# Six of eight GLU chunks as sevenfold products, mixing between pairs, and a paced LayerNorm

## The chip, the cores and the metric

One core of a Trainium2 chip runs one inference step. The metric is device time in microseconds (us) from launch to end; the kernel before takes 1117.84 us (median of 3 runs, 1117.55 to 1118.63). Engines by their names in the profile: PE (TensorE, matrix products; PEld is its weight loading), DVE (VectorE), ACT (ScalarE), POOL (GpSimd) and SP (SyncE, here only a queue that issues DMAs). Each engine executes its own instructions in the order in which the program lists them.

## The reference

Tokens are 16 meta tokens, 1024 prompt tokens and 64 sample tokens (8 sequences of 8), with 1024 channels.

```
h = RMSNorm(x);  z = h @ w_in            # 7 column groups of 1024
a_val, a_gate, a_silu, p_in, p_silu, g_a, g_b = split(z)
u = a_val * sigmoid(a_gate)                              # GLU
c = causal depthwise conv of u, width 31, history from state_conv
c = silu(LayerNorm(c)) * silu(a_silu);   br_a = c @ w_conv_out
pooled = trailing mean over 2/4/8/16 positions of p_in - p_in   (4 channel groups)
q = (pooled @ w_pool_mix per group) * pool_scale * silu(p_silu); br_b = q @ w_pool_out
y = RMSNorm(x + (sigmoid(g_a)*br_a + sigmoid(g_b)*br_b) @ w_out)
```

The ends of u and of p_in are outputs too (the new states).

## The kernel before, in words

**Products.** Channels lie on the 128 partitions, so 1024 of them are 8 chunks. Tokens lie along the free axis in two halves of 552 (8 meta, 512 prompt, 32 sample); outputs without meta tokens have 544. A half is two units of 276 or 272 columns, each in one PSUM bank. For float32 accuracy each operand is split into a high part and a low part, and a product is three matmuls: high x high, high x low, low x high. The low part is made in one of two ways. `split` (L118) casts on ACT and subtracts on DVE. `split_dma` (L123) casts and negates on ACT, and an accumulating DMA issued by POOL adds the source.

**Plain and sevenfold.** A plain block is one chunk of 128 output channels: 2 halves x 8 input chunks x 3 x 2 units = 96 matmuls. `seven` (L437) computes two output chunks x two token halves together, by a scheme of seven products in place of eight; each product has 24 matmuls, so a pair of chunks takes 168 instead of 192. It needs sums of weight blocks (`Weights.sum`, L401, on DVE), sums of input blocks (`make_t`, L690), a copy of the first product (y, L453) and two corrections on DVE (L470, L479). Loads, sums and splits of weights run 8, 5 and 4 products ahead (`prepare`, L419).

**Stages.** First six pool-input chunks are multiplied with the raw input, while the input's RMSNorm is computed. Then come 18 plain blocks (`BLOCKS`, L49): two pool inputs, and gate and value of the 8 GLU chunks. Then 16 pairs (`ORDER`, L50): pool silu (q), the two merge gates (b, a), conv silu (s). Then the mixing (L821 to L842) of the pooled chunks with `w_pool_mix`, the pool projection (L862, `ppo`), the conv projection (`pco`) and the output projection (`pwo`).

**Beside the products.** Pool windows (`pool_work`, L508) and the conv (`Conv`, L582: 31 taps of 1024 elements per chunk, then the sample part) run on DVE. They wait in a list `todo`; the planner adds estimated costs (`t_op`, L59) to one clock for DVE and a fixed time per product to one for PE, and `fill` takes items from the list until the DVE clock has caught up:

```
    def fill(until=None):
        while todo and (until is None or clock["dve"] < until):
            ...
            cost, run = todo[0].popleft()
            clock["dve"] += cost
            run()
```

`step` advances the clock of PE and runs what `defer` has put off by some steps; `spend` books other work on DVE. What is left in the list after the pairs is emitted at L816. Conv results and their sum go to DRAM (`put`, L643); the pool projection loads them again and computes the LayerNorm at fixed places between its blocks (L869 to L894): mean, centring and squares at blocks 1 to 3, variance and root at block 5, `branch_a` (L854) at blocks 5 to 7. In that stage SP issues, block by block, the load of a weight block, the load of a gate half pair `lb` and the store of the products `d_tb` (L863 to L879).

Of the kernel before, what the change touches and what calls it, by code (L numbers as in the profile page):

```python
# [43 lines left out]
NSLOT, NWS, NOP, NZ = 35, 10, 6, 8  # L44
# [4 lines left out]
BLOCKS = "p6 p7 " + " ".join(f"g{i} v{i}" for i in range(8))  # L49
ORDER = "q0 q1 q2 q3 b0 b1 b2 b3 a0 a1 a2 a3 s0 s1 s2 s3"  # L50
# [18 lines left out]
def hybrid_trunk_kernel(  # L69
# [40 lines left out]
    ones32 = const.tile([P, P], F32, name="ones32")  # L110
# [67 lines left out]
    def totals(s, n, name):  # L178
        hl = [slot(f"sum{x}_{name}", (2, n), F32R) for x in "hl"]
        split(hl[0], hl[1], s)  # L180
        out = slot(f"total_{name}", (2, n))
# [149 lines left out]
    for k in range(NK):  # L331
        dve.scalar_tensor_tensor(xs[k], xs[k], col(OFF_NG, k), rms, ALU.mult, ALU.mult)
        split_x(0, (k,), split)
    plain1(1)
    plain1(2)
    keep_raw(1, 1, outs[1])
    split_x(1, (0, 1), split)
    plain1(3)
    keep_raw(2, 1, outs[2])
    split_x(1, (2, 3), split)  # L340
    plain1(4)
    keep_raw(3, 1, outs[3])
    split_x(1, (4, 5), split)
    plain1(5)
    keep_raw(4, 1, outs[4])
    split_x(1, (6, 7), split)
# [90 lines left out]
    def seven(w, units, put):  # L437
# [46 lines left out]
    d_gate, d_sga, d_sgb, d_sa, d_c, d_tb = (  # L484
        dram.tile([NK, P, 2, H2], F32, name=f"d_{x}") for x in ("gate", "sga", "sgb", "sa", "c", "tb")
    )
    d_pool = dram.tile([NK, P, 2, 2, H2], F32, name="d_pool")
# [14 lines left out]
    def pool_load(j):  # L502
        if j < NK:
            lraw[j] = [half(f"lraw{j}{h}") for h in range(2)]
            for h in range(2):
                sp.dma_start(out=lraw[j][h], in_=d_raw[j][:, h])

    def pool_work(j):  # L508
# [3 lines left out]
        def start():  # L512
# [3 lines left out]
            sp.dma_start(out=es[:, :, :PB], in_=spool[j])  # L516
            for h in range(2):
# [11 lines left out]
            defer(2, lambda: sp.dma_start(out=o_ps[j], in_=es[:, :, DS:]))  # L529
# [10 lines left out]
        def last():  # L540
            e, es, s, ss = cur
            dve.scalar_tensor_tensor(s[:, META:], s[:, META:], 1.0 / w, e[:, META:], ALU.mult, ALU.subtract)  # L542
            dve.scalar_tensor_tensor(ss[:, :, PB:], ss[:, :, PB:], 1.0 / w, es[:, :, PB:], ALU.mult, ALU.subtract)

        def out(h):
            s, ss = cur[2:]
            o = slot(f"poolop{j}{h}", (2, H2), F32R)
            b = slice(h * DB // 2, (h + 1) * DB // 2)
            split_dma(o[:, 0, :HP], o[:, 1, :HP], s[:, META + h * HP : META + (h + 1) * HP])
            split(v3(o[:, 0, HP:], DS), v3(o[:, 1, HP:], DS), ss[:, b, PB:])  # L550
            defer(3, lambda: sp.dma_start(out=d_pool[j][:, h], in_=o.bitcast(F32)))
# [7 lines left out]
        for h in range(2):  # L559
            work.append((0.25, lambda h=h: out(h)))  # L560
# [5 lines left out]
    def gate_pair(i, base, name, func, dst):  # L566
        def put(b, h, z):
            o = z
            if not b:
                o = half2(f"z{name}{i}{b}{h}", H2)  # L570
            act.activation(o, z, func)
            act.dma_start(out=dst[2 * i + b][:, h], in_=flat(o))

        return [(w_in[base + 2 * i], w_in[base + 2 * i + 1], f"{name}{i}", UNITS2, put)]
# [3 lines left out]
    d_e = dram.tile([NK, P, TP], F32, name="d_e")  # L578
    d_es = dram.tile([NK, P, DB, DS], F32, name="d_es")


    class Conv:  # L582
        fetched = []
# [16 lines left out]
        def fetch(self):  # L600
            i = self.i
            e = self.e = slot(f"ce{i}", (CB + TP,))
            es = self.es = st.tile([P, DB, ES], F32, tag="ces", name=f"ces{i}", bufs=2)
            pool.memset(e[:, :CB], 0.0)
            sp.dma_start(out=e[:, CB:], in_=d_e[i])
            sp.dma_start(out=es[:, :, :CB], in_=sconv[i])
            sp.dma_start(out=es[:, :, CB:], in_=d_es[i])
            defer(3, lambda: sp.dma_start(out=o_cp[i], in_=e[:, TP : TP + CB]))
            defer(3, lambda: sp.dma_start(out=o_cs[i], in_=es[:, :, DS:]))
# [28 lines left out]
        def store(self):  # L638
            Conv.fetched.remove(self)
            Conv.more()  # L640
            defer(2, self.put)

        def put(self):  # L643
            sp.dma_start(out=d_c[self.i], in_=self.c)
            if not csum:
                csum.append(dram.tile([P, 2, H2], F32, name="d_csum"))
                sp.dma_start(out=csum[0], in_=self.c)
            else:
                pool.dma_start(out=csum[0], in_=self.c, accum_op=ALU.add)

    chunks = []

# [3 lines left out]
    def put_block(kind, i, h, ps):  # L656
# [7 lines left out]
        else:  # L664
            z = sg.pop(h)
            dve.tensor_tensor(v3(z, HT // 2), ps, v3(z, HT // 2), ALU.mult)
            spend(HT)
            m, p, s = parts4(z)

            def out():  # L670
                sp.dma_start(out=d_e[i][:, META + h * HP : META + (h + 1) * HP], in_=p)
# [448 lines left out]
```

## Time and profile before

| | |
|---|---|
| median of 3 runs | 1117.84 us |
| the profiled execution's own time | 1117.58 us |
| its span, first to last instruction | 1115.8 us |
| PE busy | 990.3 us, 89% |
| DVE busy | 731.9 us, 66% |
| ACT, POOL busy | 469.1 us, 174.4 us |
| granted TensorE clock, mean | 0.951 |

Busy time is the union of an engine's instructions. A row of a group of instructions gives the line, engine, operation, written tile<-read tiles, shapes and count, then busy time and mean duration, then the idle time of the engine ahead of them and what ended it. In the table by stage the busy times are those of PE, PEld, DVE, ACT and POOL in this order, each with its count of instructions in brackets. A granted clock of 1.00 is the full 2.4 GHz. In rows by time the first number is the start in us from the span's beginning, the second the length of the merged instructions.

### The profile page before, as it was taken

What the parts mean: (1) busy time and instruction counts of PE and PEld (TensorE: products, weight loads), DVE (VectorE), ACT (ScalarE), POOL (GpSimd) and SP (SyncE); (2) the same over time, 40 slices, a digit from 0 to 9 for tenths busy, and PEclk for the clock granted to TensorE, in tenths of its full rate; (3) what the DMA queues carried; (4) which work ended last, traced back from release to release, by engine and by line L of the source; (5) the groups of instructions that cost most, each with busy time, mean ns of one, the idle gap of its engine ahead of it and who ended that gap; (6) DMA issues with size and microseconds to landing.
All of it is one profiled execution on the core that took longest, in us unless ns stands there. A gap on an engine that the chain in (4) does not pass through costs nothing. (4 is left out here: it accounts for less than half of the span.)

```text
span 1115.8 us, 18229 instructions
## 1 busy us (share of the span) xinstructions
PE 990.3 (89%) x7176; PEld 962.1 (86%) x7176; DVE 731.9 (66%) x945; ACT 469.1 (42%) x791; POOL 174.4 (16%) x211
## 2 busy tenths in 40 slices
PE   9978885789999899999999999759967649999997
PEld 9978885789999899999999999758967649998885
DVE  7473542698998999999898998354434443355333
ACT  7635432313325665655455555234236452225111
POOL 0001211111213222322222232001011121000000
PEclk9999998789999999999999999979998969999999
DMA  9217999996559797989879796999346569544222
GB/s 318 73 48 165 198 214 201 205 233 162 119 143 204 171 234 185 225 200 207 197 176 239 180 224 145 309 343 320 101 107 184 161 187 279 153 155 150 77 94 95
DMA packets 144805, 205.94 MB, mean 185 GB/s; under 512 B 59216, under 2 KB 60624, under 8 KB 144720
## 3 DMA queue, kind: packets, MB, share of 16 engines
q1 hardware_dynamic: 104832, 128.42, 38.6%
q0 software_dynamic: 28368, 54.01, 28.0%
q10 hardware_dynamic: 11520, 22.35, 6.0%
q8 instruction: 56, 0.92, 0.3%
q14 instruction: 29, 0.24, 0.1%
HBM read 99.37 MB, written 55.27 MB: 139 GB/s over the span
## 5 line engine op out<-in xcount | busy, mean ns | idle before, releaser
L621 DVE SCALAR_TENSOR_TENSOR c<-ce,pv,c 128x1024 f32<-128x1024 f32 x240 | 307.9, 1283 | 5.9
L149 PE MATMUL pv<-hx,w_v 128*128 128x276 f32 x768 | 105.1, 299 | 20.7 <-DMA w_v<-raw_v 20.7
L149 PEld LDWEIGHTS pv<-hx,w_v 128*128 128x128 f32 x768 | 103.2, 197 | 21.8 <-DMA w_v<-raw_v 21.8
L149 PE MATMUL pco<-cx,w_co 128*128 128x272 f32 x768 | 101.6, 295 | 22.4 <-DMA w_co<-raw_co 11.4
L149 PEld LDWEIGHTS pco<-cx,w_co 128*128 128x128 f32 x768 | 100.1, 194 | 23.8 <-DMA w_co<-raw_co 12.1
L149 PE MATMUL pg<-hx,w_g 128*128 128x276 f32 x768 | 104.5, 298 | 14.2 <-DMA w_g<-raw_g 14.2
L149 PEld LDWEIGHTS pg<-hx,w_g 128*128 128x128 f32 x768 | 103.0, 197 | 14.9 <-DMA w_g<-raw_g 14.9
L149 PE MATMUL ppo<-q,w_po 128*128 128x272 f32 x768 | 100.0, 293 | 6.4 <-DMA w_po<-raw_po 6.0
L149 PEld LDWEIGHTS ppo<-q,w_po 128*128 128x128 f32 x768 | 99.2, 192 | 7.2 <-DMA w_po<-raw_po 6.4
L993 PE MATMUL pwo<-wo,mx 128*128 128x512 f32 x336 | 79.3, 394 | 0.0
L993 PEld LDWEIGHTS pwo<-wo,mx 128*128 128x128 f32 x336 | 63.1, 188 | 14.8
L149 PE MATMUL pp<-xg,wh_p 128*128 128x276 f32 x384 | 66.8, 296 | 7.8 <-ACT rawp L259 7.7
L149 PEld LDWEIGHTS pp<-xg,wh_p 128*128 128x128 f32 x384 | 56.5, 194 | 8.7 <-ACT rawp L259 7.9
L149 PE MATMUL pmix<-lp,m 128*128 128x272 f32 x192 | 31.5, 329 | 16.7 <-DVE lg L840 10.6
L878 DVE TENSOR_TENSOR lb<-ppo,lb 128x544 f32<-128x544 f32 x16 | 11.5, 722 | 52.0 <-DMA lb<-d_sgb 40.2
L149 PEld LDWEIGHTS pmix<-lp,m 128*128 128x128 f32 x192 | 29.6, 225 | 18.5 <-issue 10.0
L149 PE MATMUL pp<-xg,wl_p 128*128 128x276 f32 x192 | 40.7, 294 | 0.0
L663 ACT ACTIVATE zg<-pg 128x552 f32<-128x552 f32 x16 | 9.9, 628 | 68.8 <-PE pg L149 63.3
L119 ACT CAST mx<-lga 128x544 fp32r<-128x544 f32 x16 | 10.3, 646 | 61.0 <-DVE lga L954 61.0
L1012 DVE TENSOR_TENSOR xr<-pwo,xr 128x1024 f32<-128x1024 f32 (+1 forms) x9 | 10.0, 1106 | 39.4 <-DMA xr<-in_xres 24.8
L124 ACT CAST poolop<-pw 128x512 fp32r<-128x512 f32 x16 | 9.9, 618 | 60.8 <-DVE pw L542 33.1
L975 ACT ACTIVATE sq<-xr 128x1024 f32<-128x1024 f32 (+1 forms) x9 | 8.7, 965 | 63.5 <-DVE xr L1012 63.5
(328 smaller groups left out, 1918.2 us busy)
## 6 DMA issues: line engine op xcount, KB each, us to landing
d_pool<-poolop SPq DMA_DIRECT2D x16, 544.0 KB, 7.9
lp<-d_pool SPq DMA_DIRECT2D x16, 544.0 KB, 7.6
lraw<-d_raw SPq DMA_DIRECT2D x16, 276.0 KB, 7.5
d_c<-c SPq DMA_DIRECT2D x8, 544.0 KB, 5.8
lg<-d_gate SPq DMA_DIRECT2D x16, 272.0 KB, 6.1
lb<-d_sgb SPq DMA_DIRECT2D x16, 272.0 KB, 6.4
lc<-d_c SPq DMA_DIRECT2D x8, 544.0 KB, 9.1
d_tb<-lb SPq DMA_DIRECT2D x16, 272.0 KB, 2.2
```

Source lines behind the costliest of these rows:

```text
L119: act.copy(dst_h, src)
L124: act.copy(dst_h, src)
L149: pe.matmul(out[:, u, : hi - lo], w(k, a), xs(k, b)[:, lo:hi], start=first and k == ks[0] and i == 0, stop=last and k == ks[-1] and i == 2 ...
L621: dve.scalar_tensor_tensor(c, s, wk, c, ALU.mult, ALU.add)
L663: act.activation(v3(sg[h], HT // 2), ps, AF.Sigmoid)
L878: dve.tensor_tensor(of_half(lb[h]), ps, of_half(lb[h]), ALU.mult)
L975: act.activation(sq[:rows, c], xr[:, c], AF.Square, accum_out=a1 if ns[0] else a0)
L993: pe.matmul(ps[:, n - ns[0]], x(k), wo[k][n][w], start=(k == 0 and s == 0), stop=(k == NK - 1 and s == len(passes) - 1),)
L1012: dve.tensor_tensor(v3(xr[:, c], 512), ps[:, : len(ns)], v3(xr[:, c], 512), ALU.add)
```

## The change

Of the 18 plain blocks six stay: gate and value of GLU chunks 0 and 1, and the two pool inputs. The other six GLU chunks run as three pairs of gates and three of values. The pool-silu results stay in SBUF; the mixing of a group runs in four parts between the products of the next pair, and its results go through DRAM to the pool projection. Weights of plain blocks are all split by `split`. The conv chunks that finish after the pairs are kept in SBUF; the LayerNorm becomes items of the list `todo`, behind the conv. States of samples are loaded into contiguous tiles, and POOL copies them to and from the tiles with history. The copy y stands after the second product. The normalisation of the input is interleaved with the raw blocks.

```diff
-NSLOT, NWS, NOP, NZ = 35, 10, 6, 8
+NSLOT, NWS, NOP, NZ = 34, 10, 6, 11
-BLOCKS = "p6 p7 " + " ".join(f"g{i} v{i}" for i in range(8))
-ORDER = "q0 q1 q2 q3 b0 b1 b2 b3 a0 a1 a2 a3 s0 s1 s2 s3"
+BLOCKS = "g0 v0 p6 p7 g1 v1"
+ORDER = "g1 v1 g2 v2 g3 v3 q0 q1 q2 q3 b0 b1 b2 b3 a0 a1 a2 a3 s0 s1 s2 s3"
...
     plain1(1)
+    keep_raw(1, 1, outs[1])
     plain1(2)
-    keep_raw(1, 1, outs[1])
+    norm_x((0,))
+    keep_raw(2, 1, outs[2])
+    norm_x((1, 2, 3))
...
-        y = bank2(f"py_{name}")
-        act.copy(y[:, :, :n], x[:, :, :n])
-        yield
         v = bank2(f"pv_{name}")
         product_of(v, "q3", "T3", True, False)
         yield
+        y = bank2(f"py_{name}")
+        act.copy(y[:, :, :n], x[:, :, :n])
         fill(clock["pe"])
         product_of(x, "q2", "T2", False, False)
...
+            lraw[j].append(st.tile([P, DB, PB], F32, tag="pst", name=f"pst{j}", bufs=3))
+            sp.dma_start(out=lraw[j][2], in_=spool[j])
...
-            sp.dma_start(out=es[:, :, :PB], in_=spool[j])
+            stage = lraw[j][2]
...
+            pool.tensor_copy(es[:, :, :PB], stage)
+            pool.tensor_copy(stage, es[:, :, DS:])
...
+    def value_pair(i):
+        def put(b, h, z):
+            glu(2 * i + b, h, glu_gate.pop((2 * i + b, h)), z)
+            if (b, h) in ((0, 1), (1, 0)):
+                Conv(2 * i + b)
...
+            work.insert(20, (0.0, self.join))
+            work.insert(0, (0.0, self.sample_load))
...
+        def join(self):
+            i, state = self.i, self.state
+            es = self.es = st.tile([P, DB, ES], F32, tag="ces", name=f"ces{i}", bufs=1)
+            pool.tensor_copy(es[:, :, :CB], state)
+            pool.tensor_copy(es[:, :, CB:], self.new)
+            pool.tensor_copy(state, es[:, :, DS:])
+            defer(1, lambda: sp.dma_start(out=o_cs[i], in_=state))
...
-            ops[n + 1].split()
+            ops[n + 1].split(split)
+            spend(512, 2)
...
+        if mix:
+            mix.split(0)
+            mix.split_w()
+            mix.load(1)
+        if n + 1 == len(pairs):
+            for j, t in enumerate((1, 1, 2, 2, 3, 4, 5, 5)):
+                if j > 1:
+                    defer(t - 2, lambda j=j: load_q(j)) if t > 2 else load_q(j)
+                defer(t, lambda j=j: split_q(j))
+            defer(1, po[0].load)
+            defer(3, po[1].load)
+            defer(5, lambda: po[0].split(split))
         next(after, None)
         next(cur)
-        if nxt:
-            next(nxt)
+        if mix:
+            mix.gate(*mix.part(0, 0))
+        next(nxt, None)
+        if mix:
+            mix.gate(*mix.part(0, 1))
+            mix.split(1)
+        next(cur)
+        if mix:
+            mix.gate(*mix.part(1, 0))
...
-    fill()
...
+    Conv.keep = True
...
+    def centre(i):
+        if i < NK:
+            dve.tensor_tensor(conv[i], conv[i], norm["mean"], ALU.subtract)
+            norm[i] = slot("vsum" if i == 0 else f"csq{i}", (2, H2))
+            act.activation(norm[i], conv[i], AF.Square)
+        if i > 1:
+            dve.tensor_tensor(norm[0], norm[0], norm.pop(i - 1), ALU.add)
...
+    finish_a = [(5.0, root)] + [(5.2, lambda i=i: branch_a(i)) for i in range(NK)]
+    squares_ = [(2.7, lambda i=i: centre(i)) for i in range(NK + 1)]
+    squares_.append((1.3, lambda: begin_totals(0, "var", finish_a)))
+    push([(1.3, lambda i=i: sum_rest(i)) for i in range(NK)] + [(1.3, lambda: begin_totals("sum", "mean", squares_))])
...
-        (po + co)[d + 1].split()
+        (po + co)[d + 1].split(split)
+        spend(512, 2)
         for h in range(2):
             ps = gemm_half(f"ppo{d}", po[d], q, h, NK)
             dve.tensor_tensor(of_half(lb[h]), ps, of_half(lb[h]), ALU.mult)
+            spend(H2)
...
-            step(6.0)
...
+            step(2 * T_PRODUCT)
+            if d == 0:
+                load_conv(h * 4, h * 4 + 4)
+                if h:
+                    load_sum()
+            else:
+                fill(clock["pe"])
+    while todo or due:
+        fill()
+        step(0.0)
...
-            co[d + 1].split(split_dma if d < 4 else split)
+            co[d + 1].split(split)
```

## Rows read from the trace of the kernel before

**Rows 1.** Stages: window, length, busy us by engine, granted clock, DMA share, GB/s
```profile
95.50:363.00 267.50, 232.63 (x1725) 230.83 (x1726) 185.26 (x252) 86.78 (x158) 52.88 (x64) 0.94 0.89 186
363.00:713.50 350.50, 342.53 (x2690) 341.00 (x2689) 315.54 (x366) 195.22 (x325) 88.54 (x104) 0.99 0.85 201
713.50:762.00 48.50, 31.40 (x193) 29.40 (x191) 20.52 (x29) 12.56 (x21) 1.72 (x2) 0.79 0.98 352
762.00:893.80 131.80, 103.73 (x784) 102.03 (x784) 55.34 (x61) 55.90 (x74) 16.64 (x20) 0.92 0.58 166
893.80:1011.40 117.60, 101.57 (x769) 100.37 (x770) 53.59 (x76) 38.04 (x61) 11.16 (x13) 0.92 0.67 189
1011.40:1115.80 104.40, 96.40 (x416) 77.76 (x415) 42.47 (x87) 22.58 (x70) 0.00 (x0) 0.99 0.30 102
```

**Rows 2.** Waits of all engines: who, on whom, us in total, times, longest
```profile
DVE pws L537 <- DMA pes<-in_spool: 34.8, 7, 11.7
...
PE pv L149 <- DMA w_v<-raw_v: 20.7, 5, 7.9
...
PE pg L149 <- DMA w_g<-raw_g: 14.2, 3, 7.8
...
PE pmix L149 <- DVE lg L840: 10.6, 4, 9.5
```

**Rows 3.** TensorE in time, blocks and a pair: start, us, instruction
```profile
90.81 0.77 PE L149 MATMUL pp<-hx,w_p 128*128 128x276 f32 x4 [0.73 <-ACT w_p L124]
...
263.89 12.38 PE L149 MATMUL pg<-hx,w_g 128*128 128x276 f32 x96
276.11 12.38 PE L149 MATMUL pv<-hx,w_v 128*128 128x276 f32 x96
...
402.89 3.16 PE L149 MATMUL px_q<-tT,woq_q 128*128 128x272 f32 x24
...
423.99 0.78 PE L149 MATMUL px_q<-tT,woq_q 128*128 128x272 f32 x5
```

**Rows 4.** Tile c, the conv's sum: durations ns, first and last start
```profile
L634 DVE TENSOR_REDUCE c<-tap x32: 669/670/672, 266.8 to 704.6; 128x16 f32<-128x496 f32 x32
```

**Rows 5.** Groups of VectorE and ScalarE: busy us, mean ns, idle time before
```profile
L621 DVE SCALAR_TENSOR_TENSOR c<-ce,pv,c 128x1024 f32<-128x1024 f32 x240 | 307.9, 1283 | 5.9
...
L446 ACT COPY c_b<-px_b 128x544 f32<-128x544 f32 x8 | 4.9, 614 | 15.7 <-PE px_b L149 15.7
...
L479 DVE SCALAR_TENSOR_TENSOR c_b<-pv_b,c_b 128x544 f32<-128x544 f32 x4 | 2.9, 725 | 7.8 <-PE pv_b L149 7.8
...
L405 DVE TENSOR_TENSOR q_b<-q_b,a_b 128x512 f32<-128x512 f32 x4 | 2.8, 692 | 0.1
```

**Rows 6.** VectorE in time, an eviction of the pool projection and the LayerNorm's branch
```profile
799.48 0.72 DVE L878 TENSOR_TENSOR lb<-ppo,lb 128x544 f32<-128x544 f32 x1 [9.06 <-DMA lb<-d_sgb]
...
855.69 1.28 DVE L856 TENSOR_TENSOR lc<-lc,ir_c 128x1088 f32<-128x1088 f32 x1
858.34 1.36 DVE L859 TENSOR_TENSOR lc<-lc,lsa 128x544 f32<-128x544 f32 x2 [1.37 <-ACT lc L857]
...
862.88 0.73 DVE L859 TENSOR_TENSOR lc<-lc,lsa 128x544 f32<-128x544 f32 x1 [1.98 <-ACT lc L857]
...
864.96 0.72 DVE L859 TENSOR_TENSOR lc<-lc,lsa 128x544 f32<-128x544 f32 x1
```

**Rows 7.** SyncE's queue in time, the stores of block 2 of the pool projection
```profile
800.24 11.98 SPq L879 DMA_DIRECT2D d_tb<-lb  x2
```

**Rows 8.** ScalarE in time, the totals of mean and variance
```profile
773.59 1.08 ACT L119 CAST sumh_m<-lcsum 128x1088 fp32r<-128x1088 f32 x1
777.14 1.13 ACT L188 COPY total_m<-pt_m 128x544 f32<-128x544 f32 x2 [2.47 <-PE pt_m L187]
...
840.54 1.08 ACT L119 CAST sumh_v<-vsum 128x1088 fp32r<-128x1088 f32 x1
```

**Rows 9.** GpSimd's groups, the memset ahead of a conv chunk
```profile
L604 POOL MEMSET ce<- 128x30 f32 x8 | 3.3, 411 | 16.9 <-DMA poolop<-pw 9.5 <-DMA out<-pe 7.3
```

More of the change, by code (lines that the diff above doesn't have):

```diff
@@ L541, in last @@
             e, es, s, ss = cur
[L542 to L551, printed above, removed]
+            o = slot(f"pool{j}", (2, H2))
+            dve.scalar_tensor_tensor(
+                o[:, :, :HP], v3(s[:, META:], HP), 1.0 / w, v3(e[:, META:], HP), ALU.mult, ALU.subtract
+            )
+            for h in range(2):
+                c = slice(h * DB // 2, (h + 1) * DB // 2)
+                dve.scalar_tensor_tensor(
+                    v3(o[:, h, HP:], DS), ss[:, c, PB:], 1.0 / w, es[:, c, PB:], ALU.mult, ALU.subtract
+                )
+            defer(1, lambda: sp.dma_start(out=d_pool[j], in_=o))
         work = [(0.0, lambda: pool_load(j + 1)), (2 * (t_op(HP) + 0.5), start)]
@@ L569, in put @@
             if not b:
[L570 removed]
+                o = half2(f"z{name}{i}{b}{h}", n)
             act.activation(o, z, func)
[L572 to L574 removed]
+            if keep is None:
+                act.dma_start(out=dst[2 * i + b][:, h], in_=flat(o))
+            else:
+                keep[2 * i + b, h] = flat(o)
+        return [(w_in[base + 2 * i], w_in[base + 2 * i + 1], f"{name}{i}", UNITS2 if n == H2 else UNITS1, put)]
+    glu_gate, pool_gate = {}, {}
+    def value_pair(i):
[3 more added lines that the diff above has]
+                Conv(2 * i + b)
+        return [(w_in[VG + 2 * i], w_in[VG + 2 * i + 1], f"v{i}", UNITS1, put)]
     csum = []
[L578 removed]
+    d_e = dram.tile([NK, P, CB + TP], F32, name="d_e")
     d_es = dram.tile([NK, P, DB, DS], F32, name="d_es")
+    zeros = const.tile([P, CB], F32, name="zeros")
+    pool.memset(zeros, 0.0)
+    for i in range(NK):
+        sp.dma_start(out=d_e[i][:, :CB], in_=zeros)
     class Conv:
[L583 removed]
+        fetched, keep = [], False
         def __init__(self, i):
@@ L793, in hybrid_trunk_kernel, with load_q, split_q @@
     clock["t"] = 0
+    names = ORDER.split()
+    first_q = names.index("q0")
+    q, qraw = [], {}
+    def load_q(j):
+        qraw[j] = [fetch_half(d_q[j], h, f"lq{j}") for h in range(2)]
+    def split_q(j):
+        q.append([operand(f"q{j}{h}", z, split) for h, z in enumerate(qraw.pop(j))])
+        spend(H2, 2)
     cur = pairs[0][1]
-    next(cur), next(cur), next(cur)
+    next(cur), next(cur)
     after = iter(())
+    mix = None
     for n in range(len(pairs)):
-        nxt = pairs[n + 1][1] if n + 1 < len(pairs) else None
+        nxt = pairs[n + 1][1] if n + 1 < len(pairs) else iter(())
+        if mix:
[10 more added lines that the diff above has]
+            defer(5, lambda: po[0].split(split))
@@ L808, in hybrid_trunk_kernel @@
+        if n + 2 == len(pairs):
+            load_q(0)
+            load_q(1)
         next(cur)
-        if nxt:
-            next(nxt)
-        next(cur)
-        if nxt:
-            next(nxt)
+        tail = mix.part(1, 1) if mix else None
+        next(nxt, None)
+        if tail:
+            mix.gate(*tail)
+        mix = coming
         after, cur = cur, nxt
     next(after, None)
-    fill()
-    load_pooled(2)
-    load_gate(1)
-    q = []
-    for j in range(NK):
-        if j + 3 < NK:
-            load_pooled(j + 3)
-        if j + 2 < NK:
-            load_gate(j + 2)
-        if j % 2 == 0 and j < 6:
-            load_mix(j // 2 + 1)
-        if j == 4:
-            po[0].load()
-            po[0].split()
-        if j == 6:
-            po[1].load()
-        g, i = j // 2, j % 2
-        q.append([])
-        for h in range(2):
-            ps = gemm_half(
-                f"pmix{j}", lambda k, s: wm[g][:, s, k, i * P : (i + 1) * P], [pooled[2 * g], pooled[2 * g + 1]], h, 2
-            )
-            z = lgate[j][h]
-            dve.scalar_tensor_tensor(of_half(z), ps, col(OFF_PS, j), of_half(z), ALU.mult, ALU.mult)
-            q[j].append(operand(f"q{j}{h}", z, split))
-            step(1.5)
@@ new lines, in load_sum, with sum_rest, begin_totals, run @@
+    def load_sum():
+        norm["sum"] = slot("lcsum", (2, H2))
+        sp.dma_start(out=norm["sum"], in_=csum[0])
+    def sum_rest(i):
+        if not chunks[i].stored:
+            conv[i] = chunks[i].c
+            dve.tensor_tensor(norm["sum"], norm["sum"], conv[i], ALU.add)
+    def begin_totals(key, name, work):
+        parts_ = total_parts(norm[key], H2, name)
+        def run():
+            norm[name] = total_products(parts_, H2, name)
+            push(work)
+        defer(1, run)
```

200 lines of the change are left out of this document (108 added, 92 removed).

## The prediction

> **What bounds the kernel now.** I first read busy time by stage [rows 1]. The profiled execution took 1117.58 us, its span is 1115.8, so 1.8 us lie around it; the median of the runs is 1117.84, and I use the two as one. Six stages follow a start of 95.5 us: plain blocks (267.5 us), sevenfold pairs (350.5), mixing (48.5), pool projection (131.8), conv projection (117.6), output projection with its tail (104.4). TensorE is busy nearly throughout the second and the last; the gaps are in the others. So the bound is TensorE's own work in two stages, and waits in four.
>
> Who made TensorE wait comes next [rows 2]: low parts of plain weights that an accumulating DMA had not delivered (20.7 + 14.2 us in the plain blocks) and the mixing's evictions (10.6). Stall-free lengths are read where nothing waits [rows 3]: a plain block of 96 matmuls repeats every 12.22 us (263.89 to 276.11), a pair every 21.1 (402.89 to 423.99), that is 3.01 per product of 24 matmuls and 126 ns per matmul. 18 blocks of 12.22 are 220, so the plain stage holds 47.5 us of stalls and slow clock.
>
> Last, VectorE. It is busy 315.5 of 350.5 us in the pairs [rows 1], because conv taps fill its order. The planner keeps two clocks: 3.0 us per product for TensorE, and estimated costs for VectorE, whose difference is filled with taps. Summed over the code of before, it books 552 for TensorE and 545 for VectorE, so the conv should end about 7 before the pairs do; its last reduction starts at 704.6 and the pairs end at 713.5 [rows 1, 4]. The planner's books can therefore be trusted for the new order.
>
> **The change part by part.** *Start.* The input's normalisation is interleaved with the six raw blocks, but still ends in the same VectorE chain; the first block waits for that and for its own split. I start it at 90.8 us as now [rows 3], plus 1.5 of slow clock.
>
> *Plain blocks.* Six stay: 6 x 12.22 = 73.3. Their low parts come from VectorE (12 of them, 0.69 us each like the sums of [rows 5], 8 us) and wait for no DMA. Pool history is now loaded ahead through a contiguous tile, and the operands' splits leave this stage: VectorE's 34.8 us of waits on that load go [rows 2]. What is late next is VectorE itself, which has pool work here from its first microsecond. Stalls lie between 0 and the 47.5 of now; I take 6, near the low end, because the DMA behind most of them is gone.
>
> *Six pairs.* At 276 columns a product is a quarter of 12.22, 3.06; 42 of them are 128.3 us. Against twelve blocks (146.6) that is 18 less. The first pair's start costs 5.6 as now (363 to the steady rhythm). Sixteen old pairs: 16 x 21.1 = 337. The copy of the first product now stands behind the previous pair's correction; its cover is the 3.0 us product between them. I add 4 for all 22 hand-overs (0 to 55, see the third rival).
>
> *Mixing.* 192 matmuls x 126 ns = 24.2 us between pairs, instead of 48.5: the 10.6 us wait on the evictions and the wait for the first weights lie beside products. The operands' low parts move to VectorE (16 of about 0.7).
>
> These terms give the start of the pool projection: 90.8 + 1.5 + 73.3 + 6 + 5.6 + 128.3 + 337 + 24.2 + 4, and 2 for the last q operands and the first weights split after them: 673, against 762 now.
>
> *VectorE's load, which decides the rest.* The planner books 0.22 + n/960 us for n elements. By that a pair costs 5.35 (four sums and a split of 512, two corrections of 544), a conv chunk 45.35 (0.75 + 30 x 1.287 + 4 x 1.5), a pool chunk 4.1 and 1.7 for each of its 1 to 4 window steps. The new books: pool 67, conv 363, 22 pairs 118, mixing with q splits 41 (the old ones did not hold it), sums of inputs and GLU products 25, block splits 7.5: 621. TensorE's: 12 halves x 6 + 154 x 3 + 16 x 1.5 = 558. So 63 are left when the pairs end: conv chunk 7 and 0.4 of chunk 6. They run as filler in the pool projection, and the LayerNorm, queued behind them in one list, cannot begin before.
>
> *Pool projection.* Its matmuls alone are 99 us. The books offer 8 blocks x 12 less splits (12) and evictions (12.6) = 71, enough for the 63 but for none of the normalisation's own work. And the real rhythm is slower: SyncE issues the loads of a block's gates after the store of the last block's second half, and now VectorE waited 9.06 us for them after an eviction (799.48) [rows 6, 7]. Each block then costs VectorE two evictions (1.4), some 8.2 of that wait, partly filled, and 3.8 of taps behind the first: 13.4. Ahead of it stands block 0, which fills nothing while seven 544 KB loads pass; I put the first filling at 25 us and its catch-up at 38. Then 38.8 + 6 x 13.4 would be 119; a quicker load (7) makes it 109. I take 112 (99 if the loads hide, 131.8 as now): the last eviction at 785.
>
> *LayerNorm behind it.* Two chunks are added to the sum (2.6). The mean's total takes 773.59 to the end of its copies, 778.27: 4.7 [rows 8]. Centring is 8 subtractions and 7 additions, each the size of a tap (1.28, [rows 5]), squares beside them: 19.2. The variance's total and the root run from 840.54 to 855.69 less one eviction: 14.5 [rows 6, 8]. A chunk of the branch needs 2.65 to its first product (855.69 to 858.34) and 2.08 per half (862.88 to 864.96): 6.8, eight of them 54.5. Together 95.5, all serial on VectorE and ScalarE with TensorE nearly idle: the last operand at 880.5. The planner's list has nothing else to put beside it.
>
> *Conv projection.* The first half block ends 0.8 behind that; 15 halves of 6.05 follow (91). All low parts of its weights now come from VectorE, which is free; I take 5 for slow clock after the idle and rests of the stalls, where now 117.6 - 97 = 21 stand. End at 977. The output projection is untouched: 104.4. Span 1082, time 1084.
>
> *The new GpSimd copies.* 40 of them (two per pool chunk, three per conv chunk) join or move sample state. GpSimd's data work is rare now; its nearest row is the memset of 30 columns, 411 ns [rows 9]. A copy of 64 to 240 columns I bound between that and, by columns, 3.3 us. Taps took 1283 ns in the mean while GpSimd issued DMAs all along [rows 5]. In the sum the copies are 0, hidden behind 11 taps of lead and the 7 to 10% by which VectorE idles.
> The Trainium skill (SBUF — State Buffer, Who interferes with whom) says that a VectorE instruction with two SBUF inputs and a GpSimd instruction that reads SBUF block each other for a whole instruction. No run here shows it, since before has next to no such GpSimd reads; by that rule the 40 copies would be taken from VectorE's time in full, which is rival two, and by the row of the taps they cost nothing.
>
> **The rivals.** *One: the LayerNorm hides* as its name says. Then the conv projection starts at 673 + 99 = 772, and the end is 772 + 97 + 3 + 104.4, time 978. For it: VectorE is idle for 76 of 131.8 us there now [rows 1]. Against it: 63 booked us of taps stand first. A smaller remainder would only bring part of it. Chance 0.07.
>
> *Two: VectorE loses more than the books say*, by the GpSimd copies or by late loads in the pool chunks. 40 copies of 0.4 to 1.5 us are 16 to 60; the pairs' idle 7 to 10% takes up to 35 of that, the rest lengthens the chain before the LayerNorm: 1100 to 1112. Chance 0.15.
>
> *Three, slower: the hand-over between pairs.* The copy of a pair's first product on ScalarE now stands behind the correction on VectorE and its activation. Worst case: a tap just begun (1.28), the correction (0.72), an activation and the copy on ScalarE (0.61 each, [rows 5]), together 3.2 against 3.0 of cover. Now VectorE arrives early (7.8 us of waiting ahead of 4 corrections of one group [rows 5]), which leaves 1.6 in hand. If heavier orders make it arrive late, each microsecond is paid in all 21 hand-overs and again by the backlog. From 1.6 us each (33 us) the change is slower: 1119 and up, say 1130. Against it: the planner books each such job, and pays it with fewer taps. Chance 0.07.
>
> **How the numbers follow.** My forecast, a gain from plain blocks and mixing of which a serial LayerNorm returns much: 0.71, 1084 us, own range 1060 to 1103. Rival one reaches below it, two to 1112, three above. The lower bound of the unknowns is stalls 0 and pool projection 99: 1084 - 6 - 4 - 13 - 3 = 1058. Range 1058 to 1107; 0.07 below, some 0.11 above. Faster by over 0.2% (what runs of this kernel tell from nothing): forecast, rival one and nearly all of two: 0.91; slower is rival three: 0.07; the rest 0.02.
>
> **What would show it.** Right: a pool projection that starts near 673; taps until its last blocks; then about 95 us in which TensorE does nearly nothing and the chain of waits runs over VectorE's and ScalarE's LayerNorm lines; plain blocks without waits on weight DMAs; mixing matmuls amid the pairs. Wrong: taps that end before the pairs (rival one); taps longer than 1290 ns or VectorE busy above 95% in the pairs (two); TensorE waits on the first product's copy of over 1 us in each pair (three). The forecast fails if the pool projection starts after 700, or if the idle time ahead of the conv projection is below 60 or above 120 us.

## The result, and the profile after

The changed kernel takes 1084.53 us (median of 4 runs, 1083.3 to 1088.14) beside 1117.69 for the kernel before (1112.72 to 1118.63): ratio 0.9717, 95% interval 0.9681 to 0.9754. The profiled execution took 1084.14, its span is 1082.4, 33.4 less than before. The forecast was 1084. The time came about by the route forecast, but several of its terms were wrong and cancelled, so that the number fits to 1 us is luck.

The stages of the kernel after, from the table by window; its columns are those of [rows 1].

```profile
87.80:163.50 75.70, 75.68 (x577) 75.36 (x578) 55.83 (x111) 26.20 (x43) 21.39 (x21) 0.97 0.71 200
163.50:683.00 519.50, 500.33 (x3890) 495.72 (x3888) 453.23 (x548) 277.92 (x469) 135.35 (x160) 0.99 0.81 200
683.00:788.80 105.80, 98.60 (x768) 97.95 (x768) 81.97 (x100) 11.44 (x20) 0.95 (x3) 0.97 0.45 158
788.80:886.00 97.20, 23.54 (x75) 17.96 (x76) 61.71 (x67) 42.39 (x46) 0.00 (x0) 0.52 0.28 86
886.00:976.00 90.00, 90.00 (x712) 89.99 (x712) 45.05 (x67) 21.18 (x37) 0.00 (x0) 0.99 0.42 130
976.00:1082.40 106.40, 96.45 (x416) 77.77 (x414) 42.44 (x87) 22.56 (x70) 0.00 (x0) 0.97 0.29 100
```

They are the plain blocks, the 22 pairs with the mixing, the pool projection, the LayerNorm, the conv projection and the output projection. Against [rows 1]: the start is 7.7 shorter, plain blocks, pairs and mixing together 71.3 (666.5 to 595.2), the pool projection 26.0, the conv projection 27.6, the output projection 2.0 longer; and a new stage of 97.2 stands between the two projections, with TensorE busy for 23.5 of it (56 of the conv projection's 768 matmuls among its work). The sum is the 33.4. So 132.6 us were won and 97.2 of them given back in one place.

From the profile's page: busy tenths of TensorE in 40 slices of 27 us, and the granted clock.

```profile
PE   9997998999999899999999999979921359999996
...
PEclk9998999999999899999999999989965559999998
```

The hole of slices 30 to 32 is the LayerNorm. The granted clock falls behind it, to about half, with no work at stake there, and the conv projection behind it runs at 0.99.

Who made TensorE wait: total us, times, longest.

```profile
PE pco L149 <- ACT cx L119: 47.5, 8, 14.2
PE pt_var L193 <- ACT sumh_var L119: 20.2, 1, 20.2
...
PE px_q L149 <- ACT py_q L467: 6.6, 3, 2.9
PE px_g L149 <- ACT py_g L467: 4.9, 1, 4.9
...
PE px_b L149 <- ACT py_b L467: 3.0, 3, 2.2
```

The waits on weight DMAs of [rows 2] are gone from the plain blocks. In their place stand the LayerNorm's two (its variance, then the operands `cx` that the branch delivers), and the copy `y` of a pair's first product.

Why the LayerNorm starts so late is read from the conv's sum `c` (durations min/median/max ns, first and last start) and then from VectorE in time.

```profile
L663 DVE SCALAR_TENSOR_TENSOR c<-ce,pv,c x240: 1272/1285/1455, 173.1 to 776.3; 128x1024 f32<-128x1024 f32 x120
L676 DVE TENSOR_REDUCE c<-tap x32: 669/670/672, 228.9 to 782.9; 128x16 f32<-128x496 f32 x32
```

```profile
708.19 0.72 DVE L997 TENSOR_TENSOR lb<-ppo,lb 128x544 f32<-128x544 f32 x1 [10.21 <-DMA lb<-d_sgb]
708.83 10.52 DVE L663 SCALAR_TENSOR_TENSOR c<-ce,pv,c 128x1024 f32<-128x1024 f32 x8
...
788.82 0.72 DVE L997 TENSOR_TENSOR lb<-ppo,lb 128x544 f32<-128x544 f32 x1 [3.11 <-PE ppo L149]
789.47 2.60 DVE L951 TENSOR_TENSOR lcsum<-lcsum,c 128x1088 f32<-128x1088 f32 x2
...
797.22 3.70 DVE L965 TENSOR_TENSOR lc<-lc,total_mean 128x1088 f32<-128x1088 f32 x3 [2.69 <-ACT total_mean L194]
...
830.14 1.29 DVE L979 TENSOR_TENSOR lc<-lc,ir_c 128x1088 f32<-128x1088 f32 x1
...
836.95 1.28 DVE L979 TENSOR_TENSOR lc<-lc,ir_c 128x1088 f32<-128x1088 f32 x1
...
883.86 0.73 DVE L120 TENSOR_TENSOR cx<-c,cx 128x544 fp32r<-128x544 f32 x1 [0.71 <-ACT cx L119]
```

The last tap starts 93 us after the pairs ended; in [rows 4] the conv was over before they ended. Between block 0 and the first eviction of block 1 (708.19) VectorE is idle for 10.21 us while taps are pending; the first filling, which begins with eight taps, starts 25.8 us into the stage. The last eviction (788.82) is followed at once by the LayerNorm's first instruction, and from there every step waits for the one before.

### The profile page after: what moved, and what is told of

It is laid out like the page before. It is cut to its first block, busy times and chain, and to the rows that moved or that the text cites. A ratio compares the mean times of both kernels' runs of the same rounds, so it can differ in the third digit from the quotient of the medians.

```text
span 1082.4 us, 17920 instructions
## 1 busy us (share of the span) xinstructions
PE 963.5 (89%) x7032; PEld 932.5 (86%) x7032; DVE 795.6 (74%) x1043; ACT 456.1 (42%) x761; POOL 158.7 (15%) x192
## 4 chain that ended last, share of the span: by engine, by line
PE 65%; DVE 14%; ACT 9%; DMA 5%; issue 4%; SPq 1%; ACTq 1%; DVEq 0%
PE pco L149 9%; PE ppo L149 7%; PE pp L149 6%; PE px_s L149 5%; PE px_a L149 5%; PE px_q L149 4%; PE pwo L1108 4%; PE px_v L149 3%; PE px_b L149 3%; PE px_g L149 3%; PE pg L149 3%; DVE c L663 2%; PE pv_v L149 2%; DMA xr<-in_xres 2%; PE pv_g L149 1%
## 5 line engine op out<-in xcount | busy, mean ns | idle before, releaser
L149 PE MATMUL pco<-cx,w_co 128*128 128x272 f32 x768 | 108.4, 303 | 47.5 <-ACT cx L119 47.5
L119 ACT CAST mx<-lga 128x544 fp32r<-128x544 f32 x16 | 10.4, 648 | 71.4 <-DVE lga L1069 71.4
L1127 DVE TENSOR_TENSOR xr<-pwo,xr 128x1024 f32<-128x1024 f32 (+1 forms) x9 | 9.9, 1105 | 41.5 <-PE pwo L1108 25.8
L119 ACT CAST w_po<-raw_po 128x512 fp32r<-128x512 f32 x16 | 9.5, 619 | 67.7 <-DMA raw_po<-in_w_po 57.3
L1068 DVE TENSOR_TENSOR lga<-pco,lga 128x544 f32<-128x544 f32 x16 | 11.6, 724 | 33.7 <-PE pco L149 33.7
L149 PE MATMUL px_q<-tT,woq_q 128*128 128x272 f32 x192 | 29.7, 318 | 6.6 <-ACT py_q L467 6.6
L149 PEld LDWEIGHTS px_q<-tT,woq_q 128*128 128x128 f32 x192 | 28.5, 217 | 7.2 <-ACT py_q L467 7.2
L149 PE MATMUL pg<-hx,w_g 128*128 128x276 f32 x192 | 27.3, 306 | 7.0 <-ACT w_g L119 7.0
L149 PEld LDWEIGHTS pg<-hx,w_g 128*128 128x128 f32 x192 | 26.6, 203 | 7.6 <-ACT w_g L119 7.3
L149 PEld LDWEIGHTS pp<-xg,wl_p 128*128 128x128 f32 x192 | 30.2, 188 | 0.0
L149 PE MATMUL px_b<-tT,woq_b 128*128 128x272 f32 x192 | 25.6, 289 | 3.0 <-ACT py_b L467 3.0
L149 PEld LDWEIGHTS px_b<-tT,woq_b 128*128 128x128 f32 x192 | 24.5, 188 | 3.7 <-ACT py_b L467 3.7
```

Source lines behind the costliest of these rows:

```text
L119: act.copy(dst_h, src)
L149: pe.matmul(out[:, u, : hi - lo], w(k, a), xs(k, b)[:, lo:hi], start=first and k == ks[0] and i == 0, stop=last and k == ks[-1] and i == 2 ...
L1068: dve.tensor_tensor(of_half(ga), ps, of_half(ga), ALU.mult)
L1127: dve.tensor_tensor(v3(xr[:, c], 512), ps[:, : len(ns)], v3(xr[:, c], 512), ALU.add)
```

## The experiments

The kernel after gave 1084.53 in both sets of runs that held it, the kernel before 1109.8 to 1117.7 in its four, so each experiment is set against 1084.5, with its ratio to before beside it. Only the branch, block 0 and low-part experiments stood in one set with the kernel after; for the others a difference of a few us rests on the stages in the trace.

**The kernel after once more**, unedited, among later runs.

> The changed kernel unaltered, beside the next ones on the same chip: 0.972 of the kernel before in all theories (some 1079 us where before takes 1110).

Measured: 1084.53 us (1083.25 to 1084.61); the ratio is 0.9761 (0.9715 to 0.9807), since the kernel before took 1112.86 there.

**Take taps out.** Conv chunks 6 and 7 keep only their first tap.

```diff
-            work = [(t_op(SEQ) if k else 0.75, lambda k=k: self.taps(k)) for k in range(CW)]
+            taps = 1 if i > 5 else CW
+            work = [(t_op(SEQ) if k else 0.75, lambda k=k: self.taps(k)) for k in range(taps)]
```

> Leaves out 60 taps: conv chunks 6 and 7 keep only their first tap. Theory A (the taps left over when the pairs end gate the LayerNorm, which then runs alone): 77 booked us go, so nothing is left over at the start of the pool projection, the LayerNorm's list starts there, and of the 97 us ahead of the conv projection some 20 stay; 1010 us (1000 to 1030), pool projection still from about 683. Rival B (the idle stretch is set by the gates' loads and the LayerNorm's own waits, not by the taps): 1060 or more.

Measured: 1017.71 us, ratio 0.916 (0.9142 to 0.9178). The pool projection in the table by window:

```profile
687.70:810.90 123.20, 105.03 (x784) 103.32 (x784) 72.30 (x87) 47.51 (x58) 0.00 (x0) 0.93 0.51 177
```

The pairs end no earlier than in the kernel after (687.7 against 683.0), and the stage is 17 longer: the LayerNorm now lies in it, and TensorE waits there for ScalarE's casts of weights, up to 6.25 us at a time. The conv projection starts right behind it. 60 taps of 1.285 us are 77 us of VectorE's work; without them the kernel is 66.8 faster. So TensorE's stage ends where it did, and the taps decide how late the LayerNorm is.

**Move taps instead.** The planner's price of a product is raised, so that more taps are placed in the pairs.

```diff
-T_PRODUCT = 3.0
+T_PRODUCT = 3.15
```

> The planner's time for a product is 3.15 us instead of 3.0. Theory A: 154 products book 23 us more of taps before the pairs end and the plain halves 4 more, 36 instead of 63 are left, the LayerNorm begins 27 sooner, and VectorE has room (453 us busy of 519.5 in the pairs): 1060 us (1055 to 1070). Rival B (VectorE is full in the pairs in truth; each tap more delays TensorE by as much): 1080 to 1095, with the pool projection starting 20 or more later.

Measured: 1062.99 us, 0.9568 (0.9546 to 0.9591). The rows of the taps, and of pairs and pool projection:

```profile
L663 DVE SCALAR_TENSOR_TENSOR c<-ce,pv,c x240: 1272/1285/1465, 150.8 to 745.6; 128x1024 f32<-128x1024 f32 x120
```

```profile
164.00:686.70 522.70, 499.16 (x3891) 493.33 (x3889) 476.61 (x575) 279.20 (x469) 141.48 (x164) 0.99 0.81 201
686.70:796.70 110.00, 100.73 (x776) 100.08 (x776) 76.43 (x88) 22.01 (x31) 0.00 (x0) 0.95 0.45 155
```

VectorE takes 23.4 us more work into the pairs (476.61 against 453.23) and the pairs are only 3.2 longer; the last tap comes 30.7 earlier and the time falls by 21.5. One constant of the books, with all the work kept, is worth two thirds of what the whole change brought.

**Undo the sevenfold GLU alone.** Chunks 1 to 7 of the GLU become plain blocks again; all else stays.

```diff
-BLOCKS = "g0 v0 p6 p7 g1 v1"
-ORDER = "g1 v1 g2 v2 g3 v3 q0 q1 q2 q3 b0 b1 b2 b3 a0 a1 a2 a3 s0 s1 s2 s3"
+BLOCKS = "g0 v0 p6 p7 " + " ".join(f"g{i} v{i}" for i in range(1, 8))
+ORDER = "q0 q1 q2 q3 b0 b1 b2 b3 a0 a1 a2 a3 s0 s1 s2 s3"
```

> Undoes the sevenfold products of the GLU alone: chunks 1 to 7 as plain blocks, all else as after. TensorE's own account (rival C: the kernel is as long as its products): 144 matmuls more, 18 us more, 1103. Theory A (VectorE's books decide): the six pairs' sums and corrections go (32 booked), 12 blocks' splits come (18), TensorE's clock gains 18, so 31 instead of 63 are left and the LayerNorm starts 32 sooner: 18 - 32, 1070 us (1062 to 1080).

Measured: 1076.07 us, 0.9687 (0.967 to 0.9704). The pairs end 19.4 later (702.4 against 683.0), yet the last tap comes 20.5 earlier, the last operand of the conv projection 6.2 earlier (878.4), and the time is 8.5 shorter. TensorE's 18 us of saved matmuls bought nothing here: by the planner's books, the shorter time and the pairs' own sums and corrections take room for taps away. No set held this run and the kernel after together, and its ratio's interval overlaps that of the kernel after in the first set (0.9681 to 0.9754), so the 8.5 rests on these stages as much as on the times. A count of TensorE's work alone would have given a slower kernel.

**The copy y earlier.** The next pair's copy of its first product is issued ahead of the last correction of the pair before.

```diff
         act.copy(y[:, :, :n], x[:, :, :n])
+        yield
         fill(clock["pe"])
...
         nxt = pairs[n + 1][1] if n + 1 < len(pairs) else iter(())
+        next(cur)
```

> The copy of a pair's first product stands on ScalarE ahead of the previous pair's correction. Theory A (the copy behind the correction is what TensorE waits for at the hand-overs): its waits of some 16 us there go, the pool projection starts 10 to 14 sooner, the rest stays: 1073 us (1068 to 1078). Rival D (VectorE's lateness is the cause and shows again at the next correction or eviction): 1082 to 1087.

Measured: 1069.77 us, 0.9632 (0.9616 to 0.9648). The pairs with the mixing:

```profile
164.00:668.80 504.80, 493.54 (x3890) 491.25 (x3888) 453.52 (x548) 278.44 (x469) 134.85 (x160) 0.99 0.83 206
```

With the same work the stage is 14.7 shorter: idle time of TensorE falls by 7.9 (519.50 less 500.33, against 504.80 less 493.54) and its busy time by 6.8. All of it reaches the end. The edit puts the copy ahead of the correction and of the mixing's splits alike.

**The branch in two steps.** Scaling and silu of a chunk are issued ahead of the products and splits of the chunk before.

```diff
     def branch_a(i):
-        load_sa(i + 2)
...
+        if i < NK:
+            load_sa(i + 2)
+            dve.tensor_tensor(conv[i], conv[i], norm["rstd"], ALU.mult)
+            act.activation(conv[i], conv[i], AF.Silu, bias=col(OFF_LB, i), scale=col(OFF_LG, i))
+        if i == 0:
+            return
+        i -= 1
...
-    finish_a = [(5.0, root)] + [(5.2, lambda i=i: branch_a(i)) for i in range(NK)]
+    finish_a = [(5.0, root)] + [(5.2, lambda i=i: branch_a(i)) for i in range(NK + 1)]
```

> Only the order inside the LayerNorm's branch: a chunk's scaling and silu are issued before the products and splits of the chunk ahead of it. Theory A (the branch is a serial chain of VectorE and ScalarE ahead of the conv projection, 6.8 us a chunk): VectorE no longer waits for the silu and the casts, 4.2 to 4.5 us a chunk, 16 to 20 us less than the changed kernel. Rival B (TensorE or a load of the gates sets that end): under 4 us.

Measured: 1067.51 us, 0.9613 (0.9575 to 0.9652). VectorE in time, two chunks of the branch:

```profile
843.43 1.28 DVE L979 TENSOR_TENSOR lc<-lc,ir_c 128x1088 f32<-128x1088 f32 x1
...
847.89 1.28 DVE L979 TENSOR_TENSOR lc<-lc,ir_c 128x1088 f32<-128x1088 f32 x1
```

A chunk takes 4.46 in place of 6.81 (830.14 to 836.95). Seven such steps are 16.5, and the time falls by 17.0: every microsecond of the exposed branch counts.

**Fill block 0.** Taps may be placed in the pool projection's first block too.

```diff
-            else:
-                fill(clock["pe"])
+            fill(clock["pe"])
```

> Taps are also filled in during block 0 of the pool projection. Theory A: VectorE idles some 15 us there (waits of 5.3 and 10.2 us ahead of evictions), and 12 to 15 us of taps move into it, so the LayerNorm begins 8 to 12 sooner: 8 to 12 us less than the changed kernel. Rival B (the loads of the gates set the rhythm, taps or none): under 3 us.

Measured: 1074.15 us, 0.9676 (0.9636 to 0.9717); the pool projection takes 97.0 in place of 105.8, and the end comes 10.4 earlier. TensorE's longest wait in that stage of the kernel after:

```profile
727.26 61.53 PE L149 MATMUL ppo<-q,w_po 128*128 128x272 f32 x476 [6.73 <-DVE w_po L120]
```

The first filling and its evictions keep VectorE busy from 708.83 to 726.5, and the split of the next weight stands behind them. With block 0 filled, VectorE's waits ahead of the first three evictions fall from 17.1 to 9.0 (10.21 to 4.65 at the third), and TensorE's idle time in the stage from 7.2 to 0.4. So both engines win, and the 10.4 is not the price of VectorE's idle time alone.

**Low parts by DMA again**, in the plain blocks, the pool projection and the first half of the conv projection.

```diff
-            ops[n + 1].split(split)
+            ops[n + 1].split(split_dma)
...
-        (po + co)[d + 1].split(split)
+        (po + co)[d + 1].split(split_dma)
...
-            co[d + 1].split(split)
+            co[d + 1].split(split_dma if d < 4 else split)
```

> Undoes the low parts on VectorE: plain blocks, pool projection and the first half of the conv projection use the accumulating DMA again. Theory E (VectorE's low parts removed the waits of the plain stage): 6 plain blocks wait again about as before, 12 to 20 us there and 5 to 10 in the projections, 15 to 30 us more in all. Rival F (the small packets of the sample states made those DMAs late, and they are gone): 0 to 5 us more in the plain stage, and the end the same within 6, since VectorE saves 1.4 us a block of the pool projection.

Measured: 1086.93 us, 0.9793 (0.975 to 0.9835). The plain blocks take 81.5 in place of 75.7 with one wait of 3.4 on such a DMA, and the end comes 2.4 later; the pool projection gives 2.6 back (103.2), and the conv projection takes 90.0 as in the kernel after. My theory that these DMAs made the stalls of [rows 2] gave 15 to 30 at the end, and it falls; the rival, that they were late because of what else was queued, came nearer (0 to 5 in the stage, 6 at the end).

**The small packets too.** In addition the samples' states are again moved by direct strided transfers, without the contiguous tiles and GpSimd's copies.

```diff
-            sp.dma_start(out=lraw[j][2], in_=spool[j])
+            sp.dma_start(out=es[:, :, :PB], in_=spool[j])
...
-            pool.tensor_copy(es[:, :, :PB], stage)
-            pool.tensor_copy(stage, es[:, :, DS:])
...
-            sp.dma_start(out=self.state, in_=sconv[i])
-            sp.dma_start(out=self.new, in_=d_es[i])
+            sp.dma_start(out=es[:, :, :CB], in_=sconv[i])
+            sp.dma_start(out=es[:, :, CB:], in_=d_es[i])
```

> As e7_splitdma, and the sample states of pool and conv go straight to and from their strided tiles again, without the contiguous tiles and GpSimd's copies. Theory F (small packets made the accumulating DMAs of the plain stage late): TensorE's waits there return, the stage from the first block to the first pair grows from 82 us in e7_splitdma to 95 to 110, the end 10 to 25 us later than e7_splitdma's 1087. Rival G (with six blocks and the pool's operands split elsewhere the DMAs have room, whatever the packets): stage and end within 5 of e7_splitdma.

Measured: 1100.25 us, 0.9922 (0.9886 to 0.9958). Its DMA packets, its plain blocks by window, and TensorE's wait there:

```profile
DMA packets 141637, 189.60 MB, mean 173 GB/s; under 512 B 59888, under 2 KB 61296, under 8 KB 141552
```

```profile
89.20:180.30 91.10, 77.38 (x576) 76.61 (x577) 49.32 (x101) 32.40 (x53) 17.52 (x20) 0.91 0.94 195
```

```profile
PE pv L149 <- DMA w_v<-raw_v: 12.2, 1, 12.2
```

At the same bytes as in the run without this edit (189.61 MB) there are 38 thousand more packets under 512 B (59888 against 22000). The stage is 9.6 longer than there (91.1 in all, below the 95 to 110 expected), and one low part is 12.2 late. Together both edits cost 15.7 at the end. The late low part was issued late. VectorE, ScalarE and GpSimd in time:

```profile
143.63 0.34 DVE L546 TENSOR_TENSOR pws<-pes 128x176 f32<-128x176 f32 x1 [7.75 <-DMA pes<-in_spool]
...
144.65 0.65 ACT L124 CAST tT<-ts 128x552 fp32r<-128x552 f32 x1 [11.44 <-DVE ts L737]
...
161.62 0.86 POOL L126 DMA_DIRECT2D w_v<-raw_v  x1 [3.06 <-ACT tT L125]
```

TensorE stopped at 154.3. The second half of the low part was issued at 161.62 and used at 166.57, 5 us later, about what such a DMA takes (median 5.6 here, 4.7 without the edit). Ahead of it, in order, VectorE had waited 7.75 for a load of pool history that this edit again issues only where it is used, and ScalarE 11.44 for VectorE's sums behind that load. So the edit brings back small packets and late loads together, and no run parts them. The packets by themselves show in the stores of the states, here and without the edit (size, median us from issue to landing):

```profile
out<-pes SPq DMA_DIRECT2D x8, 60.0 KB, 8.3
```

```profile
out<-pst SPq DMA_DIRECT2D x8, 60.0 KB, 3.3
```

So the stall-free plain blocks come from two parts: low parts that wait for no DMA (5.8 in the stage), and states that are loaded ahead and in long runs (9.6). The second part undone alone was not run.

**All three mends and the planner's price at 3.3**: the copy y, the branch and block 0 as above.

```diff
-T_PRODUCT = 3.0
+T_PRODUCT = 3.3
...
-    def fill(until=None):
-        while todo and (until is None or clock["dve"] < until):
+    def fill(until=None, left=0):
+        while len(todo) > left and (until is None or clock["dve"] < until):
...
-            else:
-                fill(clock["pe"])
+            fill(clock["pe"], 0 if d else 1)
```

> The three mends together (copy ahead of the correction, interleaved branch, taps in block 0), and 3.3 us as the planner's time for a product. Theory A: of 63 booked us of taps 13 are left at the pool projection, the LayerNorm runs inside it, and 15 to 25 us of it stay ahead of the conv projection instead of 97: 1010 us (995 to 1022). If VectorE cannot take the taps (rival B) the pool projection starts 15 or more later and the end is above 1030.

Measured: 1019.49 us, 0.9185 (0.9166 to 0.9204): all of the computation is kept, and it beats both kernels. Its pairs, pool projection and what is left of the exposed LayerNorm:

```profile
165.40:694.30 528.90, 498.28 (x3890) 492.20 (x3888) 498.62 (x593) 281.14 (x469) 144.51 (x164) 0.99 0.80 199
694.30:793.70 99.40, 99.03 (x786) 98.82 (x787) 67.96 (x87) 39.16 (x49) 0.00 (x0) 1.00 0.56 195
793.70:818.80 25.10, 11.75 (x47) 8.95 (x46) 19.86 (x28) 11.54 (x16) 0.00 (x0) 0.60 0.67 219
```

The last tap ends at 704.5, and 25.1 us stand where 97.2 stood. The price is in the first row: VectorE is 94% busy and TensorE idles for 30.6 in the pairs, so they end 11.3 later than in the kernel after.

**The same with plain GLU chunks 1 to 7** (`BLOCKS` and `ORDER` as above).

> c1_hidden with chunks 1 to 7 of the GLU as plain blocks. Theory A: with the LayerNorm mostly hidden TensorE's products count again; 18 us more of them, 5 to 10 given back by the shorter LayerNorm rest: 5 to 15 us slower than c1_hidden. Rival H (sevenfold products of the GLU never pay here, as in e3_plain): 5 or more faster than c1_hidden.

Measured: 1037.48 us, 0.9343 (0.9321 to 0.9366), 18.0 slower, more than I expected. The last tap ends at 661.7, before the pairs do (709.7), and the conv projection starts right behind the pool projection. With taps no longer in the way, the sevenfold GLU is worth about what its matmuls save (146.6 less 128.3).

**The mends with the planner's price at 3.15.**

```diff
-T_PRODUCT = 3.3
+T_PRODUCT = 3.15
```

> c1_hidden with 3.15 us for a product instead of 3.3: 23 booked us more of taps are left, 36 in all, of which block 0 takes 10. Theory A: 10 to 20 us slower than c1_hidden, 1025 (1012 to 1035). Rival B: equal or faster, since TensorE is delayed less in the pairs.

Measured: 1024.97 us, 0.923 (0.9208 to 0.9252): 5.5 slower, less than expected. The pairs end 16.8 earlier (677.5) and the last tap 26.0 later (730.5), so it is an exchange between the two engines. Other prices were not run with the mends, and the best one is not known.

## Why the prediction was right

**Books, remainder, serial LayerNorm: right.** 63 us of taps left over when the pairs end, the first filling after 25 us, an eviction at 785 and a LayerNorm of 95.5 behind it were forecast; measured are 61.0 us of conv work behind the pairs (38 taps and two chunks' sample parts, the last tap 93 us after the pairs), 25.8, 788.8 and 95.1. Within the 95.1 the mean takes 5.2 (forecast 4.7), centring and variance 32.9 from 797.22 to 830.14 (33.7), and the branch, to the end of the last operand at 884.6, 54.5 (54.5). So rows of before priced these steps rightly, although they now stand alone, behind the pool projection and not between its blocks. The cause is shown by four doses: taps taken out (66.8), moved (21.5), a shorter branch (17.0), a filled block 0 (10.4). Rival one, that the LayerNorm hides, did not come about, but 65 of the 106 us between its 978 and the measured time were to be had, with the three mends and another constant in the books.

**Plain blocks: the size was off, and the reason half right.** They start 3 earlier than the 90.8 that I kept, and the 6 us that I left for stalls were not needed, so the pairs begin at 163.5 where my terms gave 171.6. TensorE in time (start, us, instruction):

```profile
87.80 14.92 PE L149 MATMUL pg<-hx,w_g 128*128 128x276 f32 x96 [7.03 <-ACT w_g L119]
102.56 12.35 PE L149 MATMUL pv<-hx,w_v 128*128 128x276 f32 x96
```

The first block takes 2.6 more than the second; the granted clock over it is 0.83, over the second 1.00. I gave VectorE's low parts the credit for the absent stalls; alone they are worth 5.8 in the stage and 2.4 at the end.

**Hand-over between pairs: the mis-sized term.** I added 4 us for 22 hand-overs, with a bound of 55; the experiment with the copy gives 14.7. I had compared one correction, one activation and one copy with the 3.0 of the product between, and left out that the mixing's operands are split on VectorE ahead of the correction. TensorE, VectorE and ScalarE in time at one hand-over:

```profile
322.88 3.17 PE L149 MATMUL pv_q<-tT,woq_q 128*128 128x272 f32 x24
328.03 4.80 PE L149 MATMUL px_q<-tT,woq_q 128*128 128x272 f32 x24 [1.97 <-ACT py_q L467]
```

```profile
324.17 1.36 DVE L120 TENSOR_TENSOR px<-lp,px 128x544 fp32r<-128x544 f32 x2 [1.39 <-ACT px L119]
325.45 0.69 DVE L120 TENSOR_TENSOR m<-mraw,m 128x512 fp32r<-128x512 f32 x1
326.05 0.72 DVE L489 SCALAR_TENSOR_TENSOR c_q<-pv_q,c_q 128x544 f32<-128x544 f32 x1
```

```profile
326.80 0.66 ACT L583 ACTIVATE c_q<-c_q 128x544 f32<-128x544 f32 x1 [1.60 <-DVE c_q L489]
327.37 0.61 ACT L467 COPY py_q<-px_q 128x544 f32<-128x544 f32 x1
```

The correction could start at about 323 and starts at 326.05, behind a wait of 1.39 and three splits; activation and copy follow, and TensorE has been idle since 326.06. On ScalarE, too, casts of the mixing's operands stand ahead of them. The product after the gap takes 4.80 in place of 3.17; the granted clock over it is 0.64. The mixing's matmuls lie between 338.7 and 446.3, in four pairs; the waits on this copy at those four are 1.97, 2.85, 1.73 and 2.19 us, and behind the first pair's start the longest elsewhere is 1.01. A slow product follows only the first two of these waits. The products after the second and the fourth are

```profile
359.95 5.81 PE L149 MATMUL px_q<-tT,woq_q 128*128 128x272 f32 x24 [2.85 <-ACT py_q L467]
...
422.24 3.27 PE L149 MATMUL px_b<-tT,woq_b 128*128 128x272 f32 x24 [2.19 <-ACT py_b L467]
```

The product after the third takes 3.28. The granted clock over the last three is 0.50, 1.00 and 1.00. So rival three's mechanism exists, at less than half of the 33 us from which it would have made the kernel slower. Together with the other small waits the pairs took 519.5 where my terms gave 501.1.

**Pool projection: another rhythm, and an offset.** It starts at 683.0, 10 after my 673, which my own bound of 700 allowed, and takes 105.8 in place of 112. I had counted some 8 us of waiting for the gates' load in every block. That wait stands once, ahead of block 1 (10.21). Of the later ones the longest is 0.35, and the first is

```profile
728.02 0.73 DVE L997 TENSOR_TENSOR lb<-ppo,lb 128x544 f32<-128x544 f32 x1 [0.21 <-DMA lb<-d_sgb]
```

A block takes about 11.5 in place of 13.4 there, and what lengthens the stage is the 6.73 us for which TensorE waits behind the first filling, which I had not counted. (In the prediction's sum, 7 for the load gives 112, the value taken, and not the 109 named there.) The late start and the shorter stage leave 3.8 at the last eviction. The conv projection ends at 976.0 (977 forecast): it needs none of the 5 us that I left for slow clock and stalls (91.4 from the last operand, granted clock 0.99). The output takes 106.4 (104.4). Plain blocks 8.1 short, pairs 18.4 long, pool projection 6 short and conv projection 5 short add up to nearly nothing by chance.

**Rival two: not borne out, though its rule is, in part.** VectorE is busy 453.23 of 519.50 in the pairs, 87%, and a tap has a median of 1285 ns. GpSimd's copies in time, beside taps and then with VectorE on a reduction:

```profile
599.99 0.98 POOL L648 COPY ces<-cst 128x240 f32<-128x240 f32 x1
600.91 1.23 POOL L649 COPY ces<-csn 128x64 f32<-128x64 f32 x1
...
724.82 0.39 POOL L648 COPY ces<-cst 128x240 f32<-128x240 f32 x1 [56.48 <-DVE tap L673]
725.14 0.24 POOL L649 COPY ces<-csn 128x64 f32<-128x64 f32 x1
```

The same copies take 0.39 and 0.24 there, 0.98 and 1.23 beside taps. Over all eight chunks the medians are 0.96 and 1.17, the longest 1.69 and 2.00. The Trainium skill (SBUF — State Buffer, Who interferes with whom) says that VectorE and GpSimd share one pair of SBUF ports under an exclusive lock. The trace agrees that one makes the other wait, but the wait fell on GpSimd: of 240 taps four took over 1300 ns, the longest 1455, some 0.4 us over the median in all. In the run with small packets, which has no such copies, no tap is that long:

```profile
L658 DVE SCALAR_TENSOR_TENSOR c<-ce,pv,c x240: 1273/1285/1290, 189.9 to 794.5; 128x1024 f32<-128x1024 f32 x120
```

**Open.** How the absent stalls of the plain blocks divide between low parts, packets, early loads and the new order was not separated. The gains in the two projections do not come from VectorE's low parts (103.2 and 90.0 without them); which other part brings them, and the 7.7 of the start, was not tested by itself. Nor is it known why the kernel before moves between 1109.8 and 1117.7 from one set of runs to the next while the kernel after stays.

## What to carry to other kernels

When filler work is placed by planned clocks, sum both clocks over the whole program first: what the filler's engine is short of becomes a queue ahead of whatever stands behind it in order, and a serial stage there is exposed in full. Saving matmuls on an engine whose time also covers filler work moves that work, and pays only once the rest of it is covered (some 8 us lost here, 18.0 won once most of the LayerNorm lay hidden). For a hand-over that crosses three engines, list every instruction queued ahead of it on each, the new ones of other parts of the same change too.

## What was not expected of the hardware

Stores of the samples' states took 8.3 us to land from strided tiles and 3.3 from contiguous ones, at the same 60 KB; the loads hardly differed (3.8 and 3.1). A gap of 1.97 us in TensorE's work cost another 1.6 in the product behind it, at a granted clock of 0.64, and one of 2.85 cost 2.6 at 0.50, while gaps of 1.73 and 2.19 cost nothing more, so the length of the gap alone does not tell. Over all hand-overs, idle time and longer products stand at 7.9 to 6.8. And where VectorE and GpSimd got in each other's way, it cost GpSimd up to 1.8 us a copy, and VectorE almost nothing.
